# Padding one constant tile of a hybrid-attention kernel by 32 floats, which moves every tile behind it by 128 bytes

## The chip, the core and the metric

The kernel runs on one core of a Trainium2 chip. The metric is device microseconds of one execution. Three runs of the kernel before gave 1818.48, 1817.62 and 1816.45 us; their median is 1817.62 us. One further execution was profiled. It took 1817.16 us, with a span of 1815.4 us from the first to the last instruction and a granted TensorE clock of 1.000.

## The reference

Two layers work on one sequence of 512 tokens with 1024 features. Each layer normalises, projects, runs three attention branches, gates and merges them, and then runs an MLP. Cut to what matters here:

```python
for l in range(DEPTH):                                   # 2 layers
    h = _rms_norm(x, attn_norm[l])
    proj = h @ w_in[l]                                   # 1024 x 7328
    ...                                                  # three attention branches: o_a, o_b, o_c
    gates = jax.nn.sigmoid(gate.reshape(B, S, N_BRANCH, D_MODEL))
    merged = (gates[:, :, 0] * (o_a @ wb[:DSA_OUT])
              + gates[:, :, 1] * (o_b @ wb[DSA_OUT:DSA_OUT + MLA_OUT])
              + gates[:, :, 2] * (o_c @ wb[DSA_OUT + MLA_OUT:]))
    x = x + merged @ w_out[l]                            # 1024 x 1024
    h2 = _rms_norm(x, mlp_norm[l])
    x = x + jnp.square(jax.nn.relu(h2 @ w_ff1[l])) @ w_ff2[l]   # 1024 x 4096, 4096 x 1024
```

The result must be close to float32. The kernel therefore writes each float32 operand as a rounded high half plus a low half that holds the remainder (both of type float32r), and replaces each product by three matmuls: high times high, high times low, low times high.

## The kernel before, in words

**Layout.** Activations stand transposed: 8 tiles of 128 features by 512 tokens. A weight matrix is cut into chunks of 128 x 1024 floats (512 KB). SyncE loads each chunk into a buffer `raww`; ScalarE writes its high half and VectorE its low half into a tile `hl` of 128 x 2 x 1024 (`wsplit`, L250 in the profile, since the two calls go through one helper line). Each normalised activation tile has its two halves in a tile `a4` of 128 x 2 x 512.

**The dense products.** `denseA` (L483) makes one output tile of 128 x 512 in PSUM from eight activation tiles. For each tile it issues three matmuls, with 128 columns of the weight chunk as the stationary operand and 512 columns of the activation tile as the moving one:

```python
self.nc.tensor.matmul(o, w[:, 0, c : c + P], t[:, 0], ...)   # L490: high x high
self.nc.tensor.matmul(o, w[:, 0, c : c + P], t[:, 1], ...)   # L491: high x low
self.nc.tensor.matmul(o, w[:, 1, c : c + P], t[:, 0], ...)   # L492: low x high
```

So one output tile takes 24 matmuls, and eight output tiles take 192. In the profile these rows read `psd<-a,hl` where the moving operand is an `a4` tile, and `psd<-u,hl` where it is a `u4` tile (buffer numbers are left out).

**What uses `u4`.** These tiles of 128 x 2 x 512 hold halves again. First they hold the halves of the merged, gated branches, which `w_out` is multiplied with (8 output tiles, one stretch of 192 matmuls). Then, in each of four quarters of the MLP, `w_ff1` makes eight tiles from `a4` tiles (192 matmuls, evacuated at L1322); their squared ReLU is split into `u4` tiles; and `w_ff2` makes eight output tiles from those (192 matmuls, added to `x` at L1341). A layer thus has five stretches on `u4`. In the second layer the last output tile is made in two halves of 256 columns.

**The interleaved part.** In the first half of a layer the dense projections are interleaved with the units of three attention branches (scores, transposes, outputs), in an order written out by hand. `tables` such as the identity for transposes, rope factors and masks are loaded once.

**Where tiles lie.** A tile has one address, the same in each of the 128 partitions. Pools are laid out in the order in which they are opened, and tiles within a pool in the order of their first use. The pool `cp` comes first. It holds `raww`, `x2`, `a4`, `hl`, `tmp`, `raw`, `gt` and `ot`, and all of these begin at 128 modulo 256 bytes: `a4` at 30848 + 4096 k, `hl` at 84096, 92288 and 100480. A chunk's 128-column piece lies at a multiple of 512 bytes from the start of its tile, and each low half 2048 or 4096 bytes behind its high half, so all pieces and halves have the residue of their tile. Next comes the pool `kp` with constants: `ones`, `onesr` (residue 192, at 137152), then `x0` at 137664, and behind it `gain`, `ident` (residue 0), `ropes`, `masks` and the row scales. Behind `kp` lie the pools of the stages, which reuse the same space in turn. In the program before, `u4` begins at 152064 + 4096 k, residue 0; so do `PP`, `kT` and the `SN` and `VS` of the second and third branch, and the `qT` of the second; the first branch has `kT` at residue 0 and `qT`, `SN`, `VS`, `PT` and `PR` at 128.

`x0` holds eight columns of norm weights and activation tile 0 (520 floats). It is allocated with 544 floats in `setup`.

Of the kernel before, what the change touches and what calls it, by code (L numbers as in the profile page):

```python
# [16 lines left out]
P = 128  # L17
L = 2
D = 1024
S = 512  # L20
KT = D // P
# [233 lines left out]
class Kern:  # L255
# [125 lines left out]
    def setup(self, es):  # L381
        tc, nc = self.tc, self.nc
        self.cp = es.enter_context(tc.tile_pool(name="cp", bufs=1))
        self.kp = es.enter_context(tc.tile_pool(name="kp", bufs=1))
        self.pp = es.enter_context(tc.tile_pool(name="pp", bufs=2, space=PSUM))
        self.wsetup()
        self.x = []
        k = lambda shape, nm, dt=F32: self.kp.tile(shape, dt, name=nm, tag=nm)
        self.bcol = k([96, L, 2], "bcol")
        self.warm(k)  # L390
        x0 = k([P, 4 * KT + S], "x0")[:, : KT + S]
        self.cut = KT + S // 2
        for c in (slice(0, self.cut), slice(self.cut, KT + S)):
            nc.scalar.dma_start(x0[:, c], self.ins["x0g"][:, c])
        nc.scalar.add_instruction(
            mybir.InstLoadActFuncSet(name=nc.get_next_instruction_name(), act_func_set_id=ACT_SET, ins=[], outs=[])
        )
        self.gain0 = x0[:, :KT]
        self.x.append(x0[:, KT:])
        self.wload(1)  # L400
        for j in range(1, KT):
            xt = self.t(self.cp, "x2", [P, S])
            nc.sync.dma_start(xt, self.ins["xT"][j])
            self.x.append(xt)
            if j == 1:
                self.wload(2)
        self.gain = k([P, L, NG], "gain")
        nc.sync.dma_start(self.gain, self.ins["gain"])
        self.ident = k([P, P], "ident")
        self.ropes = k([P, NROPE], "ropes")  # L410
        self.masks = k([P, NMASK], "masks", BF16)
        self.maskA = self.masks[:, C_MA : C_MA + 256]
        self.maskR = self.masks[:, C_MR : C_MR + 256]
        self.maskB = self.masks[:, C_MB : C_MB + 512]
        self.resetC = self.masks[:, C_MC : C_MC + 512]
# [993 lines left out]
```

## Time and profile before

| | |
|---|---|
| median of three runs | 1817.62 us (1816.45 to 1818.48) |
| profiled execution | 1817.16 us, span 1815.4 us |
| TensorE matmuls (PE) | busy 1803.4 us, 99% of the span, 8592 instructions |
| weight loads (PEld) | 1492.6 us, 82% |
| VectorE (DVE) | 1164.8 us, 64% |
| ScalarE (ACT) | 931.2 us, 51% |
| DMA | mean 103 GB/s |

How to read it: PE is the row of matmuls, PEld that of the weight loads, which run under the matmuls. Matmuls are pipelined: one begins before the one ahead has ended, so the duration of a row is longer than its share of the time, and what a matmul costs is the distance from its start to the next start. "Busy" of PE says that a matmul was in flight, not that the array took in a column in each cycle. A row of the timeline begins with the start and the duration in us.

### The profile page before, as it was taken

What the parts mean: (1) busy time and instruction counts of PE and PEld (TensorE: products, weight loads), DVE (VectorE), ACT (ScalarE), POOL (GpSimd) and SP (SyncE); (2) the same over time, 40 slices, a digit from 0 to 9 for tenths busy, and PEclk for the clock granted to TensorE, in tenths of its full rate; (3) what the DMA queues carried; (4) which work ended last, traced back from release to release, by engine and by line L of the source; (5) the groups of instructions that cost most, each with busy time, mean ns of one, the idle gap of its engine ahead of it and who ended that gap; (6) DMA issues with size and microseconds to landing.
All of it is one profiled execution on the core that took longest, in us unless ns stands there. A gap on an engine that the chain in (4) does not pass through costs nothing.

```text
span 1815.4 us, 23053 instructions
## 1 busy us (share of the span) xinstructions
PE 1803.4 (99%) x8592; PEld 1492.6 (82%) x8592; DVE 1164.8 (64%) x2143; ACT 931.2 (51%) x1745; POOL 32.6 (2%) x59
## 2 busy tenths in 40 slices
PE   9999999999999999999999999999999999999999
PEld 7898888878888888888888988888778888888887
DVE  8665899888865443434566568997988653434342
ACT  6646778787634232323355376686876342323231
POOL 0000000000000000000000000000000000000000
PEclk9999999999999999999999999999999999999999
DMA  5222141323352223222332222413235432233322
GB/s 191 87 82 82 61 143 53 125 78 122 130 166 93 93 94 99 97 94 93 136 106 87 82 71 79 142 52 116 82 111 168 140 93 94 93 97 100 93 94 93
DMA packets 65072, 186.72 MB, mean 103 GB/s; under 512 B 11584, under 2 KB 12480, under 8 KB 64960
## 3 DMA queue, kind: packets, MB, share of 16 engines
q1 hardware_dynamic: 58000, 178.50, 30.1%
q0 software_dynamic: 1920, 6.29, 1.0%
q8 instruction: 68, 1.11, 0.2%
q10 hardware_dynamic: 5040, 0.45, 0.2%
q14 instruction: 44, 0.36, 0.1%
HBM read 168.39 MB, written 16.78 MB: 102 GB/s over the span
## 4 chain that ended last, share of the span: by engine, by line
PE 88%; DVE 7%; ACT 3%; issue 1%; DMA 1%; SPq 0%; ACTq 0%; DVEq 0%
PE psd L492 22%; PE psd L491 22%; PE psd L490 22%; PE psd L339 3%; PE psd L338 3%; PE psd L340 3%; PE pst L786 1%; DVE SN L1001 1%; PE pss L338 1%; DVE hl L250 1%; PE pss L339 1%; PE pss L340 1%; PE pst L575 1%; PE pss L993 1%; PE pso L767 1%
## 5 line engine op out<-in xcount | busy, mean ns | idle before, releaser
L250 ACT CAST hl<-raww 128x1024 fp32r<-128x1024 f32 (+2 forms) x287 | 298.4, 1040 | 669.4 <-PE psd L492 487.3
L490 PE MATMUL psd<-a,hl 128*128 128x512 f32 x1232 | 484.2, 393 | 0.0
L491 PE MATMUL psd<-a,hl 128*128 128x512 f32 x1232 | 483.9, 393 | 0.0
L492 PE MATMUL psd<-a,hl 128*128 128x512 f32 x1232 | 483.5, 392 | 0.0
L250 DVE TENSOR_TENSOR hl<-raww,hl 128x1024 fp32r<-128x1024 f32 (+2 forms) x287 | 347.6, 1212 | 147.4 <-ACT hl L250 146.8
L490 PEld LDWEIGHTS psd<-a,hl 128*128 128x128 f32 x1232 | 231.7, 188 | 44.4
L491 PEld LDWEIGHTS psd<-a,hl 128*128 128x128 f32 x1232 | 231.7, 188 | 44.2 <-issue 0.3
L492 PEld LDWEIGHTS psd<-a,hl 128*128 128x128 f32 x1232 | 231.6, 188 | 44.2
L492 PE MATMUL psd<-u,hl 128*128 128x512 f32 (+1 forms) x648 | 254.1, 392 | 0.0
L490 PE MATMUL psd<-u,hl 128*128 128x512 f32 (+1 forms) x648 | 254.1, 392 | 0.0
L491 PE MATMUL psd<-u,hl 128*128 128x512 f32 (+1 forms) x648 | 254.1, 392 | 0.0
L1341 DVE TENSOR_TENSOR x<-x,psd 128x512 f32<-128x512 f32 x63 | 43.4, 688 | 195.3 <-PE psd L492 195.3
L490 PEld LDWEIGHTS psd<-u,hl 128*128 128x128 f32 x648 | 121.6, 188 | 28.8
L491 PEld LDWEIGHTS psd<-u,hl 128*128 128x128 f32 x648 | 121.6, 188 | 28.8
L492 PEld LDWEIGHTS psd<-u,hl 128*128 128x128 f32 x648 | 121.6, 188 | 28.8
L1322 DVE SCALAR_TENSOR_TENSOR tmp<-psd,rrep 128x512 f32<-128x512 f32 x64 | 44.3, 692 | 151.6 <-PE psd L492 151.5
L339 PE MATMUL psd<-hl,a 128*128 128x512 f32 (+3 forms) x328 | 121.0, 369 | 0.4 <-DVE hl L250 0.4
L338 PE MATMUL psd<-hl,a 128*128 128x512 f32 (+3 forms) x328 | 120.6, 369 | 0.6 <-DVE VS L250 0.5
L340 PE MATMUL psd<-hl,a 128*128 128x512 f32 (+3 forms) x328 | 120.2, 367 | 0.0
L250 ACT ACTIVATE gt<-gt 128x512 f32<-128x512 f32 x144 | 90.0, 628 | 22.2 <-DVE gt L250 18.9
L339 PEld LDWEIGHTS psd<-hl,a 128*128 128x128 f32 x328 | 67.5, 206 | 8.5 <-DVE hl L250 1.3
L338 PEld LDWEIGHTS psd<-hl,a 128*128 128x128 f32 x328 | 67.4, 206 | 8.6 <-DVE VS L250 1.0
(228 smaller groups left out, 2374.9 us busy)
## 6 DMA issues: line engine op xcount, KB each, us to landing
raww<-w SPq DMA_DIRECT2D x277, 512.0 KB, 3.5
gpark<-gt SPq DMA_DIRECT2D x48, 256.0 KB, 2.5
gt<-gpark SPq DMA_DIRECT2D x48, 256.0 KB, 3.8
x<-xT POOLq DMA_DIRECT2D x8, 256.0 KB, 4.3
park<-x POOLq DMA_DIRECT2D x8, 256.0 KB, 2.3
x<-park POOLq DMA_DIRECT2D x8, 256.0 KB, 3.7
x<-xT SPq DMA_DIRECT2D x7, 256.0 KB, 6.2
outT<-x SPq DMA_DIRECT2D x7, 256.0 KB, 2.0
```

Of the source, the lines that this page charges most:

```text
L250: return f(*a, **k)
L338: mm(ps, ah, bh, start=start, stop=False)
L339: mm(ps, ah, bl, start=False, stop=False)
L340: mm(ps, al, bh, start=False, stop=stop)
L490: self.nc.tensor.matmul(o, w[:, 0, c : c + P], t[:, 0], start=k == 0, stop=False)
L491: self.nc.tensor.matmul(o, w[:, 0, c : c + P], t[:, 1], start=False, stop=False)
L492: self.nc.tensor.matmul(o, w[:, 1, c : c + P], t[:, 0], start=False, stop=k == last)
L575: nc.tensor.transpose(ps[:d, t * P : t * P + P], y[:, t], self.ident)
L767: mm(po[a, r::4], vr[r // 2][:, r % 2, 2 * hh + g], prs[r // 2][:, c : c + P], start=False, stop=False)
L786: nc.tensor.transpose(ps[:, kt * P : kt * P + P], s[:, kt * P : kt * P + P], self.ident)
L1322: nc.vector.scalar_tensor_tensor(t, ps, 0.0, self.rrep, ALU.max, ALU.mult)
L1341: nc.vector.tensor_tensor(x, x, ps, ALU.add)
```

## The change

The tile `x0` is allocated with 576 floats in place of 544, still used only in its first 520:

```diff
-        x0 = k([P, 4 * KT + S], "x0")[:, : KT + S]
+        x0 = k([P, 8 * KT + S], "x0")[:, : KT + S]
```

(`KT` is 8 and `S` is 512.) 32 floats are 128 bytes. Everything allocated ahead of `x0`, and `x0` itself, stays where it was; everything behind it moves up by 128 bytes. In the changed program `u4` begins at 152192 + 4096 k, residue 128; `ident`, `PP`, the second and third branch's `SN` and `VS`, the second's `qT` and every `kT` get residue 128; the first branch's `qT`, `SN`, `VS`, `PT` and `PR` get residue 0. `a4`, `hl`, `x2` and `raw` stay at 128. The instructions of each engine, their order and their waits are the same, row for row, in both programs (on PE 7891 rows with equal neighbours merged). The last byte in use moves from 219648 to 219776.

## The prediction

> **What bounds the kernel now.** I first read the page's busy shares, its row of the granted clock and the chain of waits.
>
> ```profile
> PE 1803.4 (99%) x8592; PEld 1492.6 (82%) x8592; DVE 1164.8 (64%) x2143; ACT 931.2 (51%) x1745; POOL 32.6 (2%) x59
> PEclk9999999999999999999999999999999999999999
> PE 88%; DVE 7%; ACT 3%; issue 1%; DMA 1%; SPq 0%; ACTq 0%; DVEq 0%
> ```
>
> The matmuls are in flight 99% of the span at the full clock, and 88% of the chain that ended last is PE. So time can only go where a matmul starts sooner after the one ahead. The change alters no instruction, so it can act only through addresses, and the question is whether the trace shows that the spacing of matmuls hangs on where their operands lie.
>
> The next view is the busy time by stretch. The first row is the stretch of `w_out`, the second and fourth are two quarters of `w_ff2`, the third and fifth two quarters of `w_ff1`; all have 192 matmuls of 512 columns (the count includes one or two that reach over an edge).
>
> ```profile
> core 0: us, PE busy (x) PEld busy (x) DVE busy (x) ACT busy (x) POOL busy (x), PEclk, DMA share, GB/s
> 510.30:555.10 44.80, 44.80 (x194) 36.05 (x193) 25.34 (x33) 17.55 (x24) 1.37 (x3) 1.00 0.37 119
> 599.40:644.20 44.80, 44.80 (x193) 36.05 (x193) 15.96 (x17) 9.56 (x10) 0.00 (x0) 1.00 0.28 95
> 644.20:687.80 43.60, 43.60 (x194) 36.07 (x193) 19.87 (x23) 16.49 (x22) 0.00 (x0) 1.00 0.30 97
> 687.80:732.60 44.80, 44.80 (x194) 36.04 (x193) 15.98 (x17) 9.56 (x10) 0.00 (x0) 1.00 0.29 95
> 732.60:776.10 43.50, 43.50 (x194) 36.01 (x193) 19.88 (x23) 16.49 (x22) 0.00 (x0) 1.00 0.29 97
> ```
>
> PE is never idle in any of them, the clock is the same, the weight loads sum to the same 36 us, and yet the stretches on `u4` take 44.80 us where those on `a4` take 43.5 to 43.6. VectorE and ScalarE have more to do in the faster ones, so no other engine makes the difference. The timeline shows what does. Here are four matmuls inside a `w_ff1` stretch and then three inside the next `w_ff2` stretch (start, duration):
>
> ```profile
> 583.12 0.39 PE L490 MATMUL psd<-a,hl 128*128 128x512 f32 x1
> 583.35 0.39 PE L491 MATMUL psd<-a,hl 128*128 128x512 f32 x1
> 583.57 0.39 PE L492 MATMUL psd<-a,hl 128*128 128x512 f32 x1
> ...
> 584.93 0.39 PE L492 MATMUL psd<-a,hl 128*128 128x512 f32 x1
> ```
>
> ```profile
> 605.03 0.40 PE L490 MATMUL psd<-u,hl 128*128 128x512 f32 x1
> 605.27 0.39 PE L491 MATMUL psd<-u,hl 128*128 128x512 f32 x1
> ...
> 606.90 0.40 PE L492 MATMUL psd<-u,hl 128*128 128x512 f32 x1
> ```
>
> From 583.12 to 584.93 there are 8 steps, 1.81 us: 226 ns each. From 605.03 to 606.90 there are 8 steps too, 1.87 us: 234 ns each, in turn about 0.23 and 0.24. It is a settled, slower rhythm and not a stall. Both pairs of operands are of one shape and type and have the same `hl` as weights; what differs is the tile that streams. `a4` and `hl` lie at 128 modulo 256 bytes, `u4` at 0. The groups by shape say the same for all of them:
>
> ```profile
> L490 PE MATMUL psd<-a,hl 128*128 128x512 f32 x1232 | 484.2, 393 | 0.0
> L490 PE MATMUL psd<-u,hl 128*128 128x512 f32 x632 | 249.6, 395 | 0.0
> L490 PEld LDWEIGHTS psd<-a,hl 128*128 128x128 f32 x1232 | 231.7, 188 | 44.4
> L490 PEld LDWEIGHTS psd<-u,hl 128*128 128x128 f32 x648 | 121.6, 188 | 28.8
> ```
>
> A weight load lasts 188 ns in both, but ahead of one the load path idles 44.4 / 1232 = 36 ns on `a4` and 28.8 / 648 = 44 ns on `u4`. So the load itself isn't longer; the pair of streams falls into a slower step.
>
> **The change part by part.** *The ten stretches on `u4`* are the term that counts. A layer has five (`w_out` and four quarters of `w_ff2`), ten in all, 80 output tiles; the last is cut into 256-column halves, so 79 tiles x 24 = 1896 matmuls (the 632 of the row, three times). After the change `u4` is at 128, and every weight piece stands to it at a multiple of 512 bytes, as it does to `a4`. If the residue is what matters, a `w_ff2` tile gets the step of a settled `w_ff1` tile. From the stretches, cut to a tenth of a microsecond: 44.80 / 8 = 5.60 us for a tile on `u4`; on `a4` 43.50 / 8 = 5.44, which is 24 steps of 226.7 ns. The saving is 0.16 us a tile, and 79 x 0.16 = **12.6 us**. The starts give a slightly smaller one:
>
> ```profile
> 599.44 0.40 PE L490 MATMUL psd<-u,hl 128*128 128x512 f32 x1
> ...
> 644.23 0.39 PE L490 MATMUL psd<-a,hl 128*128 128x512 f32 x1
> ```
>
> ```profile
> 687.77 0.40 PE L490 MATMUL psd<-u,hl 128*128 128x512 f32 x1
> ```
>
> 44.79 us and then 43.54, a difference of 1.25 us a stretch and, over 79 / 8 stretches, 12.3 us. I take 12.6, since the first steps behind a change of operand are in the 43.54 and should go when the operands no longer differ.
>
> *What could take that back.* PE that runs ahead needs the next chunk sooner: each 5.44 us in place of 5.60. In the `w_ff1` rows VectorE is busy 19.88 of 43.50 us, ScalarE 16.49, and DMA has a share of 0.29, at just that pace and with PE never idle; in the `w_ff2` rows these engines have less to do. So the chunks come in time and this costs nothing. If that cover were gone, a late chunk would show as idle PE ahead of L490, which is 0.0 in the rows above.
>
> *The last tile*, in 256-column halves, is on the path to the end.
>
> ```profile
> 1809.48 0.28 PE L490 MATMUL psd<-u,hl 128*128 128x256 f32 x1
> ...
> 1811.61 0.28 PE L490 MATMUL psd<-u,hl 128*128 128x256 f32 x1
> ```
>
> 18 steps in 2.13 us are 118 ns, against 113 for half of 226.7. At most 48 x 5 ns = 0.2 us is to be had; I take 0.
>
> *The interleaved part.* Most pairs of operands move together (scores on `qT` and `kT`, outputs on `VS` with `PP` or `PT`, transposes of `SN`), so their difference stays. It changes from different to equal for the third branch's scores (`raw` with `kT`) and for the transposes of `raw` and `x2` with `ident`, and from equal to different for the first branch's outputs on `PR` and `x2`.
>
> ```profile
> L786 PE MATMUL pst<-ident,SN 128*128 128x128 f32 x320 | 53.9, 275 | 0.0
> L767 PE MATMUL pso<-PR,x 128*64 128x128 f32 x128 | 16.5, 277 | 0.0
> L575 PE MATMUL pst<-ident,raw 128*128 128x128 f32 x48 | 7.3, 275 | 1.3 <-DVE raw L553 1.3
> L745 PE MATMUL pst<-ident,x 128*128 128x128 f32 x64 | 9.8, 276 | 0.0
> L993 PE MATMUL pss<-kT,raw x128: 274/338/505, 321.7 to 1373.7; 128*128 128x256 f32 x64, 128*128 128x512 f32 x32, 128*128 128x384 f32 x32
> ```
>
> At 128 columns rows of equal (L786, L767) and of different residue (L745) are within 2 ns, so these moves are free: 128 outputs x 2 ns, 0.3 us at most, either way. The scores at L993 are 128 matmuls; at 7 ns each they would give 0.9 us. I take 0 for both.
>
> *A gain that I can't price* is in the dense matmuls between those units. After a break the step of `a4` and `hl`, equal residues, takes a while to settle:
>
> ```profile
> 18.08 0.50 PE L339 MATMUL psd<-hl,a 128*128 128x512 f32 x1
> ...
> 18.65 0.40 PE L338 MATMUL psd<-hl,a 128*128 128x512 f32 x1
> ...
> 20.27 0.39 PE L340 MATMUL psd<-hl,a 128*128 128x512 f32 x1
> ```
>
> That is 7 steps from 18.65 on in 1.62 us, 231 ns each, behind the matmul at 18.08 that a wait had held up. If units at the same residue break the rhythm less, some of that goes. The mean of `a4` rows is 393 ns where the settled rows above show 390: 3 ns x 3696 = 11 us is the whole of it, waits included. I think of a third at most, 3.7 us, and take 0, since the break above came from a wait with no residue in it. Downward of nothing the same term is bounded by the few pairs that now differ, 0.3 us. VectorE and ScalarE read and write the moved tiles too, but idle for more than half of these stretches.
>
> **A rule that speaks against it.** The rows above show a step that differs with the tile that streams. The Trainium skill, "TensorE: Matmul & The Clock Gate", in the section "Part 2: What happens when you issue a matmul", says that TensorE has two independent read ports, and that loading the next weights takes no read bandwidth from the running matmul. By that rule a residue is worth nothing and the sum is 0, the third case below. The trace agrees as to the overlap (188 ns loads under every matmul) and not as to equal steps (44.80 against 43.50 us).
>
> **The rivals.**
>
> *The step settles halfway, 1814 us.* Equal residues need not lock in at once; `u4` could stay at the 231 ns of the row above. Against 233.3 (44.80 / 192) that is 1.9 ns x 1896 = 3.6 us. For it: the row is of equal residues. Against it: the same operands settle at 226 in all stretches shown, and `w_ff1` does it right behind `w_ff2`.
>
> *The residue isn't the cause, 1817.6 us.* `u4` also lies higher, above 152064, where `a4` and `hl` end at 108672. If far tiles, or `w_ff2` itself, make the slow step, 128 bytes change nothing. For it: no settled stretch in the trace has its streaming tile high and at the residue of the weights, so the two can't be told apart. Against it: distance should add a delay, not a rhythm of two steps, and `w_out`, another product with other work beside it, has the same 44.80.
>
> *Equal residues meet, over 1820 us.* Two streams from the same place of a 256-byte line could collide, and `w_ff1` be spared only because both its tiles lie low. Place: the ten stretches. Price: the slowest settled step that the trace has at a like pair is in the projection that takes every fourth token as weights:
>
> ```profile
> 112.32 0.40 PE L338 MATMUL psd<-hl,a 128*128 128x512 f32 x1
> ...
> 115.14 0.40 PE L338 MATMUL psd<-hl,a 128*128 128x512 f32 x1
> 118.00:128.00 10.00, 10.00 (x44) 10.00 (x44) 6.67 (x16) 2.10 (x2) 0.00 (x0) 1.00 0.32 102
> ```
>
> 12 steps in 2.82 us are 235 ns, and there the load path is busy all the time (10.00 of 10.00 us). At 235 on `u4` it is 1.7 x 1896 = 3.2 us more, 1820.8. It decides once the step is over 233.3. Against it: every `a4` row is an equal pair and is the fast one.
>
> **How the numbers follow.** The sum is made for the profiled execution, 1817.16 us: 1817.16 - 12.6 = 1804.6. The median of the runs is 0.46 us above it, so I forecast **1805.0 us**. Chances: forecast 0.78, halfway 0.06, not the cause 0.11, meet 0.05. The forecast's own range is 1801 (with 3.7 us from the interleaved part) to 1809 (two thirds of the saving). As that alone leaves out over 2 in 10, the range reaches on to the halfway case: 1801 to 1814. A measurement of this kernel can tell about 0.2% from no change, 3.6 us; half of the halfway case falls on each side of that. Faster: 0.78 + 0.03 = 0.81. Same: 0.11 + 0.03 = 0.14. Slower: 0.05.
>
> **What would show it.** In the changed kernel's windows the stretches of `w_out` and `w_ff2` should take 43.5 to 43.6 us in place of 44.80, with 192 matmuls and PE without idle time, and the rows `psd<-u,hl` should fall from 395 to about 390 ns, with some 36 to 39 ns of idle time ahead of a load. The `w_ff1` stretches should stay at 43.5. If the `u4` stretches stay at 44.80, the residue is not the cause, wherever else time moves; if they fall and the total does not, the interleaved part has paid. If the interleaved first half of a layer (up to 510 us) changes by over 1 us, I have mispriced its pairs.

## The result and the profile after

The changed kernel takes 1804.74 us (median of 6 runs, 1804.49 to 1805.40), beside 1817.56 us for the kernel before (6 runs): a ratio of 0.9930, with a 95% interval of 0.9917 to 0.9943. The forecast was 1805.0 us. Its profiled execution took 1804.83 us with a span of 1803.0 us, 12.4 us under the 1815.4 us of before.

The busy shares and the chain, from the page of the changed kernel:

```profile
PE 1791.9 (99%) x8592; PEld 1493.6 (83%) x8592; DVE 1164.5 (65%) x2143; ACT 931.6 (52%) x1745; POOL 32.9 (2%) x59
PEclk9999999999999999999999999999999999999999
PE 87%; DVE 8%; ACT 3%; issue 1%; DMA 1%; SPq 0%; DVEq 0%; ACTq 0%
```

The same instructions, the same clock, and every other engine as busy as before to 1 us; only the matmuls are in flight for 11.5 us less. The busy time by stretch, of the changed kernel, shows where. The first row is `w_out`, the second and fourth are quarters of `w_ff2`, the third is one of `w_ff1`; each window goes from the first start of a stretch to the first start of the next.

```profile
510.33:553.85 43.52, 43.52 (x193) 36.05 (x192) 25.57 (x33) 17.57 (x24) 1.56 (x3) 1.00 0.38 120
598.20:641.72 43.52, 43.52 (x193) 36.05 (x192) 15.96 (x17) 9.60 (x10) 0.00 (x0) 1.00 0.31 97
641.72:685.24 43.52, 43.52 (x193) 36.05 (x192) 19.88 (x23) 16.49 (x22) 0.00 (x0) 1.00 0.31 97
685.24:728.76 43.52, 43.52 (x193) 36.05 (x192) 15.96 (x17) 9.60 (x10) 0.00 (x0) 1.00 0.31 97
```

All four are 43.52 us now, 192 steps of 226.7 ns; the stretches on `u4` were 44.79 us start to start. Ahead of the first `w_out` stretch there is no net change: it begins at 510.33 us where it began at 510.25. The same part of the second layer, from the end of the last `w_ff2` stretch to the start of `w_out`, takes 503.95 us where it took 503.72.

The groups by shape of the changed kernel:

```profile
L490 PE MATMUL psd<-a,hl 128*128 128x512 f32 x1232 | 484.1, 393 | 0.0
L490 PE MATMUL psd<-u,hl 128*128 128x512 f32 x632 | 245.8, 389 | 0.0
L490 PEld LDWEIGHTS psd<-u,hl 128*128 128x128 f32 x648 | 121.7, 188 | 24.6
```

A matmul on `u4` is down from 395 to 389 ns. A weight load still lasts 188 ns, and the idle time ahead of one fell from 28.8 / 648 = 44 to 24.6 / 648 = 38 ns. The rhythm of two steps is gone from the timeline. The first steps behind a change of operand are no longer slower either: the `w_ff1` stretch that took 43.54 us from its first start to the next stretch's takes 43.52, like the others. The change to `u4`:

```profile
597.98 0.39 PE L492 MATMUL psd<-a,hl 128*128 128x512 f32 x1
598.20 0.39 PE L490 MATMUL psd<-u,hl 128*128 128x512 f32 x1
598.43 0.39 PE L491 MATMUL psd<-u,hl 128*128 128x512 f32 x1
598.65 0.39 PE L492 MATMUL psd<-u,hl 128*128 128x512 f32 x1
598.88 0.39 PE L490 MATMUL psd<-u,hl 128*128 128x512 f32 x1
```

The books balance: 79 / 8 stretches x 1.27 us = 12.5 us, against 12.4 measured.

### The profile page after: what moved, and what is told of

Read it like the earlier page. It is cut to its first block, busy times and chain, and to the rows that moved or that the text cites. A ratio compares the mean times of both kernels' runs of the same rounds, so it can differ in the third digit from the quotient of the medians.

```text
span 1803.0 us, 23053 instructions
## 1 busy us (share of the span) xinstructions
PE 1791.9 (99%) x8592; PEld 1493.6 (83%) x8592; DVE 1164.5 (65%) x2143; ACT 931.6 (52%) x1745; POOL 32.9 (2%) x59
## 4 chain that ended last, share of the span: by engine, by line
PE 87%; DVE 8%; ACT 3%; issue 1%; DMA 1%; SPq 0%; DVEq 0%; ACTq 0%
PE psd L492 21%; PE psd L491 21%; PE psd L490 21%; PE psd L339 3%; PE psd L340 3%; PE psd L338 3%; PE pst L786 1%; DVE SN L1001 1%; PE pss L338 1%; DVE hl L250 1%; PE pss L340 1%; PE pss L339 1%; PE pst L575 1%; PE pso L767 1%; PE pso L338 1%
## 5 line engine op out<-in xcount | busy, mean ns | idle before, releaser
L490 PE MATMUL psd<-a,hl 128*128 128x512 f32 x1232 | 484.1, 393 | 0.0
L492 PE MATMUL psd<-a,hl 128*128 128x512 f32 x1232 | 483.4, 392 | 0.0
L490 PEld LDWEIGHTS psd<-a,hl 128*128 128x128 f32 x1232 | 231.8, 188 | 44.0
L492 PEld LDWEIGHTS psd<-a,hl 128*128 128x128 f32 x1232 | 231.5, 188 | 44.2
L491 PE MATMUL psd<-u,hl 128*128 128x512 f32 (+1 forms) x648 | 250.4, 386 | 0.0
L492 PE MATMUL psd<-u,hl 128*128 128x512 f32 (+1 forms) x648 | 250.4, 386 | 0.0
L490 PE MATMUL psd<-u,hl 128*128 128x512 f32 (+1 forms) x648 | 250.4, 386 | 0.0
L492 PEld LDWEIGHTS psd<-u,hl 128*128 128x128 f32 x648 | 121.7, 188 | 24.7
L490 PEld LDWEIGHTS psd<-u,hl 128*128 128x128 f32 x648 | 121.7, 188 | 24.6
L491 PEld LDWEIGHTS psd<-u,hl 128*128 128x128 f32 x648 | 121.7, 188 | 24.6
```

The lines of the kernel that those rows point to most:

```text
L490: self.nc.tensor.matmul(o, w[:, 0, c : c + P], t[:, 0], start=k == 0, stop=False)
L491: self.nc.tensor.matmul(o, w[:, 0, c : c + P], t[:, 1], start=False, stop=False)
L492: self.nc.tensor.matmul(o, w[:, 1, c : c + P], t[:, 0], start=False, stop=k == last)
```

## The experiments

The change moves every tile behind `x0` at once, and the profile alone can't say which pair, which distance and which period count. Four theories stood: the difference in residue between `u4` and the weights; another moved tile; the residue 128 itself; the far place of `u4`.

**One part alone.** The kernel before, with only `u4` moved:

```diff
                 self.fp = fctx.__enter__()
+                nc.gpsimd.memset(self.fp.tile([P, 32], F32, name=f"pad{l}", tag="pad"), 0.0)
```

> The kernel before with 128 bytes put only in front of the u4 tiles (a tile of 32 floats ahead of them in their own pool, one memset a layer); ident, kT, PP, SN, VS and the rest stay at their old places. Theory (the residue of u4 against the weights is all that counts): the stretches of w_out and w_ff2 take 43.5 us in place of 44.80 and the run takes 1804.5 to 1805.5 us. Rival (one of the other moved tiles, or the constants, carries part of it): the u4 stretches stay at 44.80 us, or fall while the total stays above 1806 us.

Measured: 1804.48 us (4 runs), before 1817.07 (7 runs); ratio 0.9933, interval 0.9916 to 0.9949. A quarter of `w_ff2` and one of `w_ff1`, by stretch:

```profile
597.78:641.30 43.52, 43.52 (x193) 36.05 (x192) 15.96 (x17) 9.60 (x10) 0.00 (x0) 1.00 0.31 97
641.30:684.82 43.52, 43.52 (x193) 36.05 (x192) 19.88 (x23) 16.49 (x22) 0.00 (x0) 1.00 0.31 97
```

So `u4` carries the whole effect; `ident`, `kT`, `PP`, `SN` and `VS` have no measurable part in it.

**256 bytes further.**

```diff
-        x0 = k([P, 8 * KT + S], "x0")[:, : KT + S]
+        x0 = k([P, 640], "x0")[:, : KT + S]
```

> The changed kernel with x0 at 640 floats: every tile behind it lies another 256 bytes higher, so u4 keeps 128 modulo 256 but goes from 128 to 384 modulo 512. Theory with a period of 256 bytes: no change, 1804.7 us within 0.7, u4 stretches 43.5 us. Rival with a period of 512 bytes (the length of a weight piece): u4 stretches back to 44.80 us, about 1817 us.

Measured: 1804.51 us (2 runs), interval of the ratio 0.9911 to 0.9951; a `w_ff2` stretch:

```profile
598.08:641.60 43.52, 43.52 (x193) 36.05 (x192) 15.96 (x17) 9.59 (x10) 0.00 (x0) 1.00 0.31 98
```

A distance of 256 bytes is as good as 0, so the period of the free place isn't 512. A longer one would show as steps of different length within one output tile, since its weight pieces step by 512 bytes themselves; in the changed kernel's trace all 192 steps of the stretch from 598.20 us on are 226 or 227 ns.

**Everything at 0.** 128 bytes in front of the first pool of the changed kernel:

```diff
         self.cp = es.enter_context(tc.tile_pool(name="cp", bufs=1))
+        nc.gpsimd.memset(self.cp.tile([P, 32], F32, name="pad", tag="pad"), 0.0)
```

> The changed kernel with 128 bytes in front of everything: a4, hl, u4, raw, kT and PP all go from 128 to 0 modulo 256, so all differences stay. Theory (the difference counts): 1804.7 us within 0.7, all stretches 43.5 us. Rival (residue 128 itself is the good place): w_ff1 and w_ff2 stretches both at 44.80 us; 64 w_ff1 tiles and 79 u4 tiles at 0.16 us each make at least 1827 us.

Measured: 1804.57 us (2 runs), interval of the ratio 0.9912 to 0.9951. `w_ff2` and `w_ff1`:

```profile
597.96:641.48 43.52, 43.52 (x194) 36.05 (x192) 15.96 (x17) 9.60 (x10) 0.00 (x0) 1.00 0.31 97
641.48:685.00 43.52, 43.52 (x194) 36.05 (x192) 19.88 (x23) 16.49 (x22) 0.00 (x0) 1.00 0.31 97
```

Neither 0 nor 128 is the good residue in itself: with all three tiles at 0 the step is the same, so it is the difference that counts.

**The weights alone.** In the changed kernel only `hl` goes to residue 0:

```diff
+            pad = lambda s: self.nc.gpsimd.memset(self.cp.tile([P, 32], F32, name=s, tag=s), 0.0)
+            if i == 0:
+                pad("pad0")
             hl = self.t(self.cp, "hl", [P, 2, 1024], F32R)
+            if i == 0:
+                pad("pad1")
```

> The changed kernel with hl alone moved by 128 bytes, to residue 0, between a4 and u4 that both stay at 128 (two small tiles, one ahead of hl and one behind it). Theory (the difference between the streaming tile and the weights counts, for any pair): the a4 stretches go to 44.80 us as well as the u4 stretches; 143 tiles at 0.16 us make 22.9 us and the dense matmuls of the interleaved part some more: 1828 to 1845 us. Rival (only tiles that lie far from the weights suffer): w_ff1 stays at 43.5 us and only the u4 stretches go back, 1817 us.

Measured: 1834.60 us (2 runs), ratio 1.0097, interval 1.0076 to 1.0117. The stretches of `w_out`, `w_ff2` and `w_ff1`, and then everything ahead of the first `w_out`:

```profile
514.81:559.61 44.80, 44.80 (x194) 36.04 (x192) 25.29 (x32) 17.29 (x24) 1.07 (x2) 1.00 0.36 113
604.93:649.55 44.62, 44.62 (x194) 36.18 (x193) 15.97 (x17) 9.54 (x10) 0.00 (x0) 1.00 0.30 95
649.55:694.17 44.62, 44.62 (x193) 36.17 (x192) 19.91 (x23) 16.48 (x22) 0.00 (x0) 1.00 0.30 95
...
0.00:514.81 514.81, 510.78 (x2562) 424.29 (x2563) 411.86 (x876) 343.93 (x719) 15.04 (x30) 1.00 0.33 109
```

`w_ff1`, whose tiles all lie low and which had been fast in every trace, is as slow as `w_ff2`; the theory of far tiles had it stay at 43.5 us. The size is a little off: 44.62 and not 44.80 us in the MLP, that is 232.4 ns a step and not 233.3. The interleaved part of the first layer is 4.5 us longer (514.81 against 510.33). Most of its matmuls are of `a4` and `hl`, the pair that this edit drew apart.

**How far is near enough.** The changed kernel with a small tile ahead of `u4` alone, of another size in each layer, so that one run gives two distances:

```diff
                 self.fp = fctx.__enter__()
+                nc.gpsimd.memset(self.fp.tile([P, (8, 16)[l]], F32, name=f"pad{l}", tag="pad"), 0.0)
```

(Then 24 and 40, 48 and 56, 32 and 96 floats. The edit stands in the code of a layer; the lines around it are left out.)

> The changed kernel with a small tile ahead of u4 alone, so that u4 lies 32 bytes past the residue of the weights in the first layer and 64 in the second; all else stays equal to the weights. The settled step on u4 is 226.7 ns at distance 0 and 233.3 at the old distance. Theory A (any distance other than 0 costs the same): both layers' u4 stretches 44.8 us, 1817 us in all. Theory B (the cost grows with the distance up to 128 bytes): 43.8 us in the first layer and 44.1 in the second, 1809 us. Theory C (only 128-byte blocks count): 43.5 us in both, 1804.7 us.

> As before with distances 96 (first layer) and 160 bytes (second). Theory A: 44.8 us in both layers, 1817 us. Theory B: 44.5 us in both, 1814 us. Theory C: 43.5 us at 96 and 44.8 at 160, 1811 us.

> As before with distances 192 (first layer) and 224 bytes (second). Theory A: 44.8 us in both, 1817 us. Theory B: 44.1 us at 192 and 43.8 at 224, 1809 us. Theory C: 44.8 us in both, 1817 us.

> As before with distances 128 (first layer) and 384 bytes (second, the old place modulo 512). With a period of 256 bytes both are the old case: u4 stretches 44.80 us in both layers, settled step 233.3 ns, 1817 us. With a period of 512 the first layer can differ from the second; the run that moved the weights alone gave 232.6 ns a step at 128 and not 233.3, so that 44.65 us in the first layer beside 44.80 in the second would say that the cost, though not the free place, has the longer period.

Measured, one run each: 1815.31, 1818.49, 1817.58 and 1817.58 us, beside 1818.93 us for one run of the kernel before on that chip. One `w_ff2` stretch of each layer, by stretch. First, distances 32 and 64:

```profile
601.20:646.01 44.81, 44.81 (x194) 35.99 (x192) 15.95 (x17) 9.57 (x10) 0.00 (x0) 1.00 0.30 95
1503.39:1547.35 43.96, 43.96 (x193) 36.06 (x192) 15.96 (x17) 9.57 (x10) 0.00 (x0) 1.00 0.31 96
```

Distances 96 and 160:

```profile
599.52:644.33 44.81, 44.81 (x193) 36.04 (x192) 15.98 (x17) 9.54 (x10) 0.00 (x0) 1.00 0.30 95
1502.76:1547.74 44.98, 44.98 (x194) 36.16 (x193) 15.95 (x17) 9.57 (x10) 0.00 (x0) 1.00 0.32 95
```

Distances 192 and 224:

```profile
599.68:644.48 44.80, 44.80 (x194) 35.91 (x193) 15.96 (x17) 9.57 (x10) 0.00 (x0) 1.00 0.30 95
1502.47:1547.27 44.80, 44.80 (x193) 36.07 (x192) 15.96 (x17) 9.55 (x10) 0.00 (x0) 1.00 0.32 95
```

Distances 128 and 384:

```profile
599.48:644.27 44.79, 44.79 (x193) 36.03 (x192) 15.97 (x17) 9.57 (x10) 0.00 (x0) 1.00 0.29 95
1502.51:1547.30 44.79, 44.79 (x193) 36.04 (x192) 15.96 (x17) 9.57 (x10) 0.00 (x0) 1.00 0.32 95
```

Theory B (cost by distance) and theory C (blocks of 128 bytes) fall: 32 bytes cost as much as 128. Theory A holds for six of the seven distances (384 is 128 once more, modulo 256), where the stretch is 44.8 to 45.0 us; 64 is the exception with 43.96. These are single runs, but the five `u4` stretches of a layer agree to 0.02 us in each of their traces. 128 and 384 agree to 0.01 us, which fits a period of 256 bytes for the cost too; as 384 lies 128 short of 512, a cost with a period of 512 that is the same on both sides of equal isn't excluded by this pair. The 44.62 us of the run that moved the weights isn't a matter of this distance alone: `u4` and `hl` were 128 apart there, and `hl` itself had moved.

**The exception, and less than 32 bytes.** Distance 64 in the first layer, and 16 in the second (buffers of `u4` made 256 bytes longer, and used from their fifth float on in the second layer; left out here are the two places that take their tile from this function, and the small tile ahead of the buffers, of 16 floats in the first layer and 64 in the second):

```diff
+    def u4(self, l):
+        t = self.t(self.fp, "u4", [P, 2 * S + 64], F32R)
+        c = (0, 4)[l]
+        return t[:, c : c + 2 * S].rearrange("p (a s) -> p a s", a=2)
```

> The changed kernel with u4 alone at a distance of 64 bytes from the weights' residue in the first layer and 16 bytes in the second (buffers 256 bytes longer, used from a start of 16 bytes in). If the cheaper 43.96 us at 64 came from the distance and not from the second layer, where it was seen, the first layer's stretches are now 43.96 us; otherwise 44.80. At 16 bytes: 44.80 us if any distance costs, 43.52 if less than 32 bytes is near enough; under 43.52 would be a better place than equal.

Measured: 1811.32 us (one run; before 1816.84, 7 runs).

```profile
598.35:642.31 43.96, 43.96 (x194) 36.05 (x192) 15.96 (x17) 9.54 (x10) 0.00 (x0) 1.00 0.30 96
1497.68:1542.16 44.48, 44.48 (x194) 36.10 (x193) 15.97 (x17) 9.59 (x10) 0.00 (x0) 1.00 0.33 96
```

The cheaper 64 is a matter of the distance, since it came again in the other layer to 0.01 us. 16 bytes cost 0.96 us a stretch: near isn't near enough. For these stretches no distance tried is better than 0.

**The interleaved part made equal.** Two more small buffers in the first branch's pool take its tiles to 128 again:

```diff
-        dg=1, raw=2, qT=2, kT=2, SN=9, PT=2, VS=1, PR=2, st=6, mx=8, PP=2, sq=2,
+        dg=1, raw=2, qT=2, kT=2, SN=9, PT=2, VS=1, PR=2, st=8, mx=8, PP=2, sq=2,
```

> The changed kernel with two more small buffers (st 8 in place of 6, 128 bytes) in the first branch's pool: its qT, SN, VS, PT and PR go from residue 0 back to 128, so that now every large tile that TensorE reads lies at 128. Theory (pairs in the interleaved part don't settle, so their residues are worth next to nothing): 1804.2 to 1805.0 us, no change from the changed kernel. Rival (the breaks between dense matmuls get shorter where the units share the residue): 1801 to 1803.5 us, gained ahead of the first w_out stretch.

Measured: 1804.34 us (1803.70 to 1806.32, 4 runs; before 1816.84, 7 runs), ratio 0.9935, interval 0.9918 to 0.9952.

```profile
0.00:509.64 509.64, 504.63 (x2563) 422.92 (x2563) 411.41 (x876) 343.43 (x718) 14.97 (x28) 1.00 0.34 109
509.64:553.16 43.52, 43.52 (x194) 36.04 (x192) 25.33 (x33) 17.57 (x24) 1.35 (x3) 1.00 0.38 121
```

It can't be told from the changed kernel: the intervals overlap, and the 0.7 us by which this execution reached `w_out` earlier (509.64 against 510.33) is less than its runs differ among themselves. It is no proven gain, so the changed kernel remains the version to use.

## Why the prediction was right, step by step

**What bounds.** The reading that an equal shape and equal weights with a slower step left the place of the streaming tile as the cause is shown by the run with `u4` alone, and that it is its place against the weights by the runs with everything at 0 and with the weights alone.

**The ten stretches.** Predicted 12.6 us; by the traces 1.27 us a stretch, 12.5 us. The choice of the settled step (226.7 ns) over the starts (12.3 us) was right: the first steps behind the change of operand went, too. The 12.6 has a little of rounding in it (0.16 us a tile, where the traces give 1.27 / 8 = 0.159).

**What could take that back.** Nothing did: the rows of L490 have 0.0 us of idle time ahead of them, and VectorE is busy for 15.96 of 43.52 us in a `w_ff2` stretch.

**The last tile.** Taken as 0, with a gain of up to 0.2 us as its bound. It went a little the other way. The steps of its 256-column matmuls in the changed kernel:

```profile
1796.88 0.28 PE L491 MATMUL psd<-u,hl 128*128 128x256 f32 x1
...
1799.04 0.28 PE L491 MATMUL psd<-u,hl 128*128 128x256 f32 x1
```

18 steps in 2.16 us, 120 ns and steady, against 118 of before: 0.1 us lost over 48. So the bound, half of a 512-column step, was drawn from the wrong rule: at equal places the step grows by 226.7 - 120 = 106.7 ns from 256 columns to 512, not by half of 226.7. And equal places are not the best ones at this width. At distance 16, in the second layer of the run with 64 and 16, 18 such steps take 2.04 us, 113 ns (L497 is that kernel's L492):

```profile
1800.91 0.28 PE L497 MATMUL psd<-u,hl 128*128 128x256 f32 x1
...
1802.95 0.28 PE L497 MATMUL psd<-u,hl 128*128 128x256 f32 x1
```

In the traces with 64, 160, 224 and 384 in the second layer these steps are 117 to 119 ns; only in the run with the weights moved alone, at 128, are they 120 again. So at 256 columns every distance that `u4` alone was moved to is faster than 0, by 1 to 5%, and the rule of the long stretches doesn't carry over.

**The interleaved part.** Taken as 0, with up to 3.7 us of gain as a bound. The first layer's came out at 510.33 against 510.25 us, and making all of its residues equal moved it by less than the noise. The reason given, that the break shown came from a wait with no residue in it, fits; it was not isolated. The same part did lose 4.5 us when `hl` and `a4` came apart, so it isn't insensitive to the places of its dense pair; of the small pairs that moved, none shows a price (the outputs on `PR` and `x2` go from equal to different and stay at a mean of 277 ns). Two steps of that paragraph don't hold. The 11 us that the bound of 3.7 was taken from is a difference of durations, and what a matmul costs is the distance of starts: by that the 3696 matmuls of `a4` stand 233 ns apart in the mean (by the starts in the trace of before, waits included, against 226.7 settled), so there was more to be had in principle, some 23 us. And that VectorE and ScalarE idle for more than half holds for the MLP stretches, but not for VectorE in `w_out` (busy 25.34 of 44.80 us), nor for either ahead of it (411 and 344 of 510 us in the changed kernel). This did no harm: writing a half of `u4` takes VectorE 692 ns and ScalarE 622 ns before and after.

**The rivals.** *Halfway* fell: the step is 226.7 from the first matmul of a stretch. *Not the cause* fell with the run that moved `u4` alone, and its form with far tiles with `w_ff1` at 44.62 us when all its tiles lay low. *Equal residues meet* fell with every trace. I had given the three 0.22 together. The evidence against *not the cause* was weaker than it looked: that `w_out` and `w_ff2` are equally slow speaks against `w_ff2` itself, but both stream the same high tiles, so it left the far place open; and a rhythm of two steps is no sign by itself, since at a distance of 192 the step is as slow without one. The choice of the residue over the height was a judgement that the trace before could not settle, and the runs did.

**The rule weighed there.** The rows first: 36 us of weight loads in 192 steps, and stretches of 43.52 or 44.80 us by the place of the streaming tile alone. The Trainium skill, "TensorE: Matmul & The Clock Gate", "Part 2: What happens when you issue a matmul", gives the two streams independent read ports. The runs agree that the loads overlap, and differ in that the streams do disturb each other, by 3% of a step.

## What to carry to other kernels

Where two kinds of stretches have the same matmuls and one of them has a slower settled step, with PE never idle, look at where the streaming tile and the weights lie before looking at other engines. For dense float32r matmuls of 128 x 512 with a new weight load each, let both tiles begin at the same place modulo 256 bytes; any other place tried cost 1 to 3.4%, 16 bytes off included. A pad for this is free, but it belongs right ahead of the tile that needs it: in a shared pool every later constant moves it again.

Two limits of this stand in the traces. At 256 columns equal places gave the slowest step of those tried, 120 ns. And equal places are not enough for the projection that takes every fourth token as weights: its tiles lie at the same residue in the changed kernel, as before, and its step is still slow, 12 steps in 2.84 us or 237 ns:

```profile
112.23 0.40 PE L338 MATMUL psd<-hl,a 128*128 128x512 f32 x1
...
115.07 0.40 PE L338 MATMUL psd<-hl,a 128*128 128x512 f32 x1
```

## What the runs showed that was not expected

- At 512 columns the cost is nearly a switch and not a slope: 43.52 us a stretch at distances 0 and 256, 44.48 at 16, and 44.79 to 44.98 at 32, 96, 128, 160, 192, 224 and 384, but 43.96 at 64, twice. Why 64 is cheaper isn't settled.
- The slow step isn't one rhythm. At a distance of 128 the durations of the matmuls alternate between 0.39 and 0.40 us and the steps between 0.23 and 0.24, as the rows in the prediction show. At 192 all durations are the same, in the first layer of that run, and the mean step is as long:

```profile
610.18 0.39 PE L490 MATMUL psd<-u,hl 128*128 128x512 f32 x1
610.41 0.39 PE L491 MATMUL psd<-u,hl 128*128 128x512 f32 x1
610.64 0.39 PE L492 MATMUL psd<-u,hl 128*128 128x512 f32 x1
610.88 0.39 PE L490 MATMUL psd<-u,hl 128*128 128x512 f32 x1
```

- At 256 columns the order turns round: 120 ns a step at distance 0, 117 to 119 where `u4` alone was moved to 64, 160, 224 and 384, and 113 at 16. Why isn't known.
- With the weights moved alone, the same pair of tiles settled at 44.80 us for `w_out` and 44.62 us for the MLP. So the slow step has more than one settled form, and what picks it is open, as is the mechanism inside the chip: the runs show that the distance between the streaming tile and the weights decides between the fast and the slow step, and not which part makes one stream wait for the other.
